# Mixer factors kept unsplit in DRAM, builder rows scaled on GpSimd, the pool pair's weights ahead of the norm of v, down's first activations in weight buffers

## The chip, the cores and the metric

One Trainium2 chip, of which the kernel uses one core. The time is device microseconds of one execution. Three runs of the kernel before took 2842.69, 2843.27 and 2844.00 us (median 2843.27).

## The reference

One decoder layer over 2048 prompt rows and 32 sample rows (8 sequences of 4), width D = 1024, all in f32:

```python
xn = rmsnorm(x)
proj = xn @ w_in        # u | v (512 each) | pool input (256) | queries (256) | 3 gates (1024 each)
u, v = split(gelu(a_part));  vn = layernorm(v)
br_a = (u * chunk_spatial(vn)) @ w_branch_a      # causal 128x128 mixing
br_b = pooled(pool_input) @ w_pool * scale @ w_branch_b   # windows 2, 4, 8, 16
br_c = cross_attn(q, mem_k, mem_v) @ w_branch_c  # 256 memory tokens
merged = sum(sigmoid(gate_i + b_i) * br_i)
h = x + rmsnorm(merged @ w_out)
g, up = split(rmsnorm(h) @ w_up)                 # 2816 each
out = h + rmsnorm((gelu(causal_conv3(g)) * up) @ w_down)
```

It also returns the memory keys and values, the pool and conv states and the normalised v of the sample rows.

## The kernel before

**Precision.** Each f32 operand is kept as a high and a low part (fp32r). `split_half` (L108) makes them: a ScalarE cast (L113) and a VectorE subtraction (L114). A product is then three matmuls: high x high, high x low, low x high. Weights arrive through `load_raw` (`rawp`, four buffers of 4 KB a partition) and are split into a ring of `u` tiles.

**Products in blocks.** The products with w_in and w_up are done as two-by-two block products with seven multiplications in place of eight (`blocks`, L392 and after; products 1, 6, 2, 7, 4, 5, 3). The right factors come from the weights: `right_factors` (L350) builds sums `sm` on VectorE (L359 to L364) and writes them to DRAM for later blocks, where `kept_factors` reads them. The left factors, named 1 to 8, are sums of transposed rows, made by a *builder* ahead of time. Product 1 leaves PSUM by a ScalarE copy to a tile `t` (L406), the others through VectorE (L410, L416).

**Stages.** The mixer handles four blocks of 512 prompt rows (block 1 also has the sample rows, `SB`), and for each: the values projection (`tok_mm`, L136 to L138, into `psv`), its GELU on ScalarE, the layer norm of v (bn_stats L633, bn_aggr L635, the reciprocal root on GpSimd L143 and L145, then L637 and L638 on VectorE), the pool pair (`pair(2 * AW)`, the first block product), pooling, queries and attention, the u part with its spatial gating (which reads the normalised v), and the gates: four steps with three gate products each and the branch products. Then `outproj` multiplies by w_out in two column halves of four rounds, each of which loads and splits a piece of w_out. After the four blocks come the up projection in two halves of the rows (its activations go to DRAM, `act`) and the down projection.

**The builder.** `mix_steps(b + 1)` and `ffn_items` are generators that `next(steps)` moves on once per gate product. An item (`pair_steps`) fetches pieces of two row tiles into a tile `fx` (SP's DMA, L247), scales each by its row's reciprocal root (L249, ScalarE), transposes them on TensorE (L233), takes the gains on ScalarE (L235, L236) and forms the sums on VectorE (L224 to L227). It then stores the factors to DRAM: three of them unsplit (`mf_`, L260), and the other five for the mixer as high and low parts (ScalarE copy `xh` L265, VectorE L266, four DMAs L268 and L270 to `md` and `m8`). There are 28 items for the mixer (24 of 128 rows, 4 of 16) and 36 for the feed-forward part. `load_block` loads a block's factors ahead of `outproj`: five tiles already split, and three that it splits (L304, L305). The tiles `fx`, `xh`, `t`, and others come from one pool, `w4`, of four buffers.

**Down.** Groups of two activations are loaded by `load_acts` into tiles `ar` of a pool `ra` (L1134), split (L1135 ScalarE, L1136 VectorE) and multiplied with w_down. The pool `ra` is opened when the pools of up are closed.

**Order.** A scheduler sets each engine's order when the program is built; engines then run in that order. One SP queue issues the loads and stores.

Of the kernel before, what the change touches and what calls it, by code (L numbers as in the profile page):

```python
# [50 lines left out]
def decoder_step(ctx: ExitStack, tc: tile.TileContext, A: dict, O: dict):  # L51
# [186 lines left out]
    def pair_steps(items, gains, spare=None):  # L238


        def fetch(e):
            rows, n, k = items[e][:3]
            pool, tag = (spare, "fx") if spare and e % 2 else (w4, "w4")
            f = pool.tile([P, D], F32, name="fx", tag=tag)
            for i, (src, r) in enumerate(rows):
                part = f[:n, 512:D].rearrange("p (h t c) -> p h t c", h=2, t=2)[:, :, i]
                DMA.dma_start(part, src.rearrange("p (h k c) -> p h k c", h=2, k=4)[:, :, k])  # L247
                if r is not None:
                    S.activation(part, part, AF.Copy, scale=r)  # L249
            return f  # L250

        nxt = fetch(0)
        yield
        for e, (rows, n, k, split, sums) in enumerate(items):
            f = nxt
            if e + 1 < len(items):
                nxt = fetch(e + 1)
            pair_cols(f, [f[:n, 512 + q * P:512 + (q + 1) * P] for q in (0, 2, 3, 1)], n, gains, k)
            pair_sums(f, n)
            DMA.dma_start(sums, f[:, 5 * n:8 * n].rearrange("p (i c) -> p i c", i=3))  # L260
            yield
            m = (4 + (len(split) > 1)) * n
            fa = f[:, 0:m]
            h = w4.tile([P, D], F32R, name="xh", tag="w4")[:, 0:m]
            S.copy(h, fa)  # L265
            V.tensor_tensor(fa.bitcast(F32R), fa, h.bitcast(F32), ALU.subtract)  # L266
            for hl, src in enumerate((h.bitcast(F32), fa)):
                DMA.dma_start(split[0][hl], src[:, 0:4 * n].rearrange("p (i c) -> p i c", i=4))  # L268
                if len(split) > 1:
                    DMA.dma_start(split[1][hl], src[:, 4 * n:5 * n])  # L270

    def ffn_items(b):
        s = b // 2
        pairs = [[(hd[r], rt[:, r:r + 1]) for r in (b * 4 + j, b * 4 + 2 + j)] + [P, (b % 2) * (xw[s] - 256) + j * P]
                 for j in range(2)]
        if b == 2:
            pairs.append([(hns[0:16], None), (hns[16:32], None), 16, 256])
        return [((r1, r2), n, k, [[xd[s][:, :, k // 2, hl, k % 2, c0:c0 + n] for hl in range(2)]],
                 xf[s][:, :, k, c0:c0 + n]) for r1, r2, n, c0 in pairs for k in range(4)]
# [8 lines left out]
    def mix_steps(b):  # L288

        for r1, r2, n, _ in mix_rows(b):  # L290
            for src, i in (r1, r2):
                xt = w4.tile([P, D], F32, name="xt", tag="w4")
                DMA.dma_start(xt[:n], src)
                row_rstd(xt[:n], n, rx[:n, i:i + 1])
            yield
        items = [([(src, rx[:n, i:i + 1]) for src, i in (r1, r2)], n, k,
                  [[md[b][:, k, hl, :, c0:c0 + n] for hl in range(2)], [m8[b][:, hl, k, c0:c0 + n] for hl in range(2)]],
                  mf_[b][:, :, k, c0:c0 + n]) for r1, r2, n, c0 in mix_rows(b) for k in range(4)]
        yield from pair_steps(items, gx)
# [7 lines left out]
    def load_block(b, own=None):  # L307

        X = own or {"A": []}
        if own is None:  # L310
            for k in range(4):
                X["A"].append(hb([P, 2, 4, mw[b]], name="xa"))
                DMA.dma_start(X["A"][k].bitcast(F32), md[b][:, k])
            X[8] = hb([P, 2, 4, mw[b]], name="x8")
            DMA.dma_start(X[8].bitcast(F32), m8[b])
        for i in (6, 5, 3):
# [3 lines left out]
        return X  # L320

    def factor(X, i):

        if "A" in X:
            return (lambda k, hl: X["A"][k][:, hl, XS.index(i)]) if i in XS else (lambda k, hl: X[i][:, hl, k])
        return lambda k, hl: X[i][k // 2][:, hl, k % 2]
# [127 lines left out]
    with ExitStack() as mctx, ExitStack() as m2ctx:  # L454
# [138 lines left out]
        def mixer(b, X, steps):  # L593
# [7 lines left out]
            def pair(c, each=None):  # L601
                W = kept_factors(c) if b else right_factors(w_in, c)
                for _, _, (h, *it) in all_blocks(W, X, [(0, w)], False, each):
                    yield (h, *it)
# [12 lines left out]
            for k in range(4):  # L617
                wr = raw3(v_first if b + k == 0 else load_raw(w_in[:, k:k + 5:4, AW:2 * AW]), 2)
                u = split_unit(wr)
                for ti, (h, c0, n) in enumerate(tts):  # L620
                    for k2 in range(2):
                        lh, ll = ((X["A"][k][:, hl, (0, 1)[k2] if h == 0 else 2] if h == 0 or k2 else X[8][:, hl, k])
                                  [:, c0:c0 + n] for hl in range(2))
# [5 lines left out]
            for ti, (h, c0, n) in enumerate(tts):  # L629
                vv = vn[:, ti] if n == P else w2.tile([P, NTB], F32, name="vg", tag="w2")[:n, 0:AW]  # L630
                S.activation(vv, psv[ti][:n], AF.Gelu_apprx_tanh)
                bs = stat.tile([P, 6], F32, name="bs", tag="bs")
                V.bn_stats(bs[:n], vv)  # L633
                ba = stat.tile([P, 2], F32, name="ba", tag="ba")
                V.bn_aggr(ba[:n], bs[:n])  # L635
                r = rstd_of(ba[:n, 1:2], n)
                V.scalar_tensor_tensor(vv, vv, ba[:n, 0:1], C["lng"][:n], ALU.subtract, ALU.mult)  # L637
                V.scalar_tensor_tensor(vv, vv, r, C["lnb"][:n], ALU.mult, ALU.add)  # L638
                vns.append(vv)
                if n < P:  # L640
                    DMA.dma_start(O["new_gmlp_v"].rearrange("l b t c -> (l b t) c")[16 * h:16 * h + 16], vv)
# [20 lines left out]
            for h, j, ps, add, op, sp in pair(2 * AW):  # L662
# [3 lines left out]
                for dst, sl, m in parts:  # L666
# [198 lines left out]
        def outproj(b, mg, steps=None, then=None):  # L865
# [10 lines left out]
            if steps:  # L876
                steps()
            ss2 = [stat.tile([P, 2], F32, name="sso", tag="sso") for _ in range(nt)]
            for ch in range(2):
# [111 lines left out]
        for k in range(4):  # L991
            f2 = hb([P, 2176], F32, name="fx")
            for j in range(2):
# [8 lines left out]
                DMA.dma_start(mf_[0][:, :, k, c0:c0 + P], f[:, 640:D].rearrange("p (i c) -> p i c", i=3))  # L1002
        X = load_block(0, X)
        for b in range(NB):
# [6 lines left out]
            if b < NB - 1:  # L1011
                nxt = {}
                outproj(b, mg, lambda: nxt.update(load_block(b + 1)))
                X = nxt
# [84 lines left out]
    with ExitStack() as fctx:  # L1099
# [19 lines left out]
        def down_all(s, pending):  # L1119
# [150 lines left out]
```

## Time and profile before

| | |
|---|---|
| median of three runs | 2843.27 us |
| the profiled execution | 2840.73 us |
| its span | 2838.9 us |
| mean granted TensorE clock | 0.985 |
| TensorE matmuls busy | 2727.1 us, 16833 instructions |
| VectorE busy | 2052.0 us, 3928 |
| ScalarE busy | 1310.6 us, 2510 |
| GpSimd busy | 111.8 us, 201 |
| HBM read, written | 336.32 MB, 104.18 MB |

The profile is of one execution. Engines are PE (TensorE's matmuls), PEld (its weight loads), DVE (VectorE), ACT (ScalarE), POOL (GpSimd) and SP (SyncE, which issues DMAs). A busy time is a sum over instructions; instructions of one engine overlap a little. In brackets behind a row of a timeline stands the idle time of the engine before it and what ended it. The block stages lie in the span as follows: the gates of blocks 0 to 3 at 195 to 325, 560 to 695, 895 to 1040 and 1195 to 1320 us; the pool pair and what follows the norm of v at 46 (block 0), 402 (1), 772 (2) and 1100 us (3); the output projection after block 0 and the values projection of block 1 at 325 to 402; up from 1450; down from 2317.

### The profile page before, as it was taken

Reading aid. Unit: us, or ns where it says so; the run is one execution under the profiler, and the core shown is the slowest. Engines: PE = TensorE matmul, PEld = TensorE weight load, DVE = VectorE, ACT = ScalarE, POOL = GpSimd, SP = SyncE. Lnnn points to the kernel's source line nnn. Section 1 sums busy time; section 2 is a strip of 40 time slices with the busy share of each in tenths; the row PEclk is TensorE's granted clock in tenths of the full one; section 3 lists DMA queues with packets and bytes.
Section 4 is the critical chain, followed back from the end, with each engine's and each line's share of the span. In section 5 each row is a group of like instructions: output and inputs, shape, how many; then the busy total and the mean of one; then the engine's idle time right before and its main releaser. Section 6 shows DMA issues by size and latency. Waiting matters only on the chain.

```text
span 2838.9 us, 45265 instructions
## 1 busy us (share of the span) xinstructions
PE 2727.1 (96%) x16833; PEld 2417.1 (85%) x16833; DVE 2052.0 (72%) x3928; ACT 1310.6 (46%) x2510; POOL 111.8 (4%) x201
## 2 busy tenths in 40 slices
PE   7999999999999999999999999999999989999998
PEld 5788878899889888989778788899999978888887
DVE  7788758477487667877587777767777757668665
ACT  5565446465466555756454433433333333115112
POOL 2010020000000001000000000000000000001001
PEclk9999999999999999999999999999999999999999
DMA  6457744586646774577744422442222244225312
GB/s 217 146 192 235 232 165 139 159 239 211 222 135 207 226 257 173 168 211 229 266 144 124 148 89 85 140 167 83 68 76 83 68 175 141 90 74 201 100 70 91
DMA packets 454639, 443.39 MB, mean 156 GB/s; under 512 B 32533, under 2 KB 385322, under 8 KB 450442
## 3 DMA queue, kind: packets, MB, share of 16 engines
q1 hardware_dynamic: 454418, 440.49, 47.9%
q8 instruction: 133, 2.18, 0.3%
q14 instruction: 88, 0.72, 0.1%
HBM read 336.32 MB, written 104.18 MB: 155 GB/s over the span
## 4 chain that ended last, share of the span: by engine, by line
issue 49%; PE 10%; DMA 2%; DVE 2%; ACT 1%; POOL 1%; SPq 0%; POOLq 0%; DVEq 0%; ACTq 0%
PE mm L388 5%; PE mm L136 1%; PE mm L138 1%; PE mm L137 1%; POOL rs L143 1%; PE mm L133 1%; PE mm L132 1%; PE mm L131 1%; DMA xd<-xh 1%; DMA fx<-hd 1%; POOL rs L145 1%; DMA m<-xh 0%; ACT tp L158 0%; DVE u L114 0%; ACT u L113 0%
## 5 line engine op out<-in xcount | busy, mean ns | idle before, releaser
L113 ACT CAST u<-raw 128x512 fp32r<-128x512 f32 x884 | 536.8, 620 | 949.6 <-PE mm L138 330.4
L388 PE MATMUL mm<-X,u 128*128 128x512 f32 (+2 forms) x5544 | 896.0, 323 | 7.5 <-ACT u L113 2.2
L388 PEld LDWEIGHTS mm<-X,u 128*128 128x128 f32 x5544 | 801.7, 189 | 93.7 <-DVE t L447 5.6
L114 DVE TENSOR_TENSOR u<-raw,u 128x512 fp32r<-128x512 f32 x884 | 597.8, 688 | 209.0 <-ACT u L113 203.0
L388 PE MATMUL mm<-xa,u 128*128 128x256 f32 (+1 forms) x3072 | 436.7, 294 | 21.5 <-ACT t L406 15.4
L388 PEld LDWEIGHTS mm<-xa,u 128*128 128x128 f32 x3072 | 399.0, 195 | 35.8 <-ACT t L406 20.6
L388 PE MATMUL mm<-xs,u 128*128 128x256 f32 (+1 forms) x2304 | 332.1, 291 | 20.0 <-ACT u L113 11.1
L388 PEld LDWEIGHTS mm<-xs,u 128*128 128x128 f32 x2304 | 300.3, 194 | 33.7 <-ACT u L113 14.0
L1148 DVE TENSOR_TENSOR Y<-Y,mm 128x512 f32<-128x512 f32 x268 | 183.2, 686 | 110.6 <-PE mm L138 109.9
L136 PE MATMUL mm<-u,a 128*128 128x512 f32 x616 | 242.9, 394 | 8.9 <-ACT a L1135 8.9
L138 PE MATMUL mm<-u,a 128*128 128x512 f32 x616 | 245.8, 399 | 0.0
L137 PE MATMUL mm<-u,a 128*128 128x512 f32 x616 | 244.9, 398 | 0.0
L136 PEld LDWEIGHTS mm<-u,a 128*128 128x128 f32 x616 | 117.8, 191 | 36.0 <-ACT a L1135 9.3
L137 PEld LDWEIGHTS mm<-u,a 128*128 128x128 f32 x616 | 116.5, 189 | 27.0
L138 PEld LDWEIGHTS mm<-u,a 128*128 128x128 f32 x616 | 116.3, 189 | 26.7 <-DVE a L1136 1.1
L114 DVE TENSOR_TENSOR u<-sm,u 128x512 fp32r<-128x512 f32 x120 | 82.8, 690 | 48.0 <-ACT u L113 46.5
L1072 DVE SCALAR_TENSOR_TENSOR d<-gE,vecs,d 128x1024 f32<-128x1024 f32 x88 | 112.7, 1280 | 5.7 <-ACT d L1070 5.2
L113 ACT CAST u<-sm 128x512 fp32r<-128x512 f32 x120 | 74.4, 620 | 86.2 <-PE mm L388 67.2
L416 DVE TENSOR_TENSOR t<-mm,t 128x256 f32<-128x256 f32 (+2 forms) x130 | 61.2, 471 | 63.3 <-PE mm L388 62.4
L143 POOL TENSOR_SCALAR rs<-ss 128x1 f32<-128x1 f32 (+2 forms) x57 | 33.8, 593 | 1734.6 <-ACT tp L158 1734.0
L136 PE MATMUL mm<-u,mg 128*128 128x512 f32 x224 | 88.8, 396 | 0.6 <-ACT mix L897 0.6
L138 PE MATMUL mm<-u,mg 128*128 128x512 f32 x224 | 88.2, 394 | 0.0
(300 smaller groups left out, 3764.0 us busy)
## 6 DMA issues: line engine op xcount, KB each, us to landing
raw<-in_w_in SPq DMA_DIRECT2D x96, 512.0 KB
raw<-ws SPq DMA_DIRECT2D x96, 512.0 KB
raw<-in_w_up SPq DMA_DIRECT2D x88, 512.0 KB
raw<-in_w_down SPq DMA_DIRECT2D x44, 512.0 KB
raw<-in_w_out SPq DMA_DIRECT2D x32, 512.0 KB
raw<-in_w_in SPq DMA_DIRECT2D x48, 256.0 KB
act<-d SPq DMA_DIRECT2D x22, 528.0 KB
ar<-act SPq DMA_DIRECT2D x22, 528.0 KB
```

The lines of the kernel that those rows point to most:

```text
L113: S.copy(uv[:, 0], src)
L114: V.tensor_tensor(uv[:, 1], src, uv[:, 0].bitcast(F32), ALU.subtract)
L131: T.matmul(ps, lhsT=uk[:, 0], rhs=xk(xT, k, 0, c0, n), start=i == 0, stop=False)
L132: T.matmul(ps, lhsT=uk[:, 0], rhs=xk(xT, k, 1, c0, n), start=False, stop=False)
L136: T.matmul(ps, lhsT=lh, rhs=wh, start=first, stop=False)
L137: T.matmul(ps, lhsT=lh, rhs=wl, start=False, stop=False)
L138: T.matmul(ps, lhsT=ll, rhs=wh, start=False, stop=last)
L143: G.tensor_scalar(r[:n], ms, more, EPS, ALU.add, ALU.add)
L388: T.matmul(ps, lhsT=u[:, wl, k], rhs=x(k, xl)[:, c0:c0 + n], start=not more and k + i == 0, stop=k + i == 5, skip_group_check=True)
L416: V.tensor_tensor(v7, pc, v, ALU.add)
L1072: V.scalar_tensor_tensor(d[j][:, 0:FSB], gE[j][:, k:k + FSB], cw(k, f), d[j][:, 0:FSB], ALU.mult, ALU.add)
L1148: return V.tensor_tensor(yd, yd, ps, ALU.add)
```

## The change

It has four parts.

*Factors unsplit in DRAM.* `md` holds all eight factors of a mixer block unsplit, in the order `MI`, and a mixer item stores them by one DMA (L259 of the new kernel). `xh` and its subtraction go for the mixer's items. `load_block` is now a generator: it loads the eight tiles one by one and splits each (L302, L303 of the new kernel); `outproj` moves it on after each of its eight weight splits, seven tiles early (six in block 1's), and the rest at its end.

*Row scale on GpSimd.* L249 becomes a GpSimd `tensor_scalar` (L247 of the new kernel): 112 instructions of 128 rows and 8 of 16.

*Pool pair ahead of the norm.* The pool pair's weights are taken before the norm of v, and the norm stands behind the pool pair in the program.

*Activations.* The first group of activations of down's first half is loaded through `load_raw` and not into `ra`.

```diff
-    md = [hdp.tile([P, 4, 2, 4, mw[b]], F32, name=f"md{b}") for b in range(NB)]
-    m8 = [hdp.tile([P, 2, 4, mw[b]], F32, name=f"m8{b}") for b in range(NB)]
-    mf_ = [hdp.tile([P, 3, 4, mw[b]], F32, name=f"mf{b}") for b in range(NB)]
+    md = [hdp.tile([P, 8, 4, mw[b]], F32, name=f"md{b}") for b in range(NB)]
...
-                    S.activation(part, part, AF.Copy, scale=r)
+                    G.tensor_scalar(part, part, r, None, ALU.mult)
...
+            if split is None:
+                DMA.dma_start(sums, f[:, 0:8 * n].rearrange("p (i c) -> p i c", i=8))
+                yield
+                continue
...
-    def load_block(b, own=None):
+    MI = (1, 2, 4, 7, 8, 5, 6, 3)
+
+    def load_block(b, X, order, early):
...
+        def load(i):
             X[i] = hb([P, 2, 4, mw[b]], name="xs")
-            DMA.dma_start(X[i][:, 1].bitcast(F32), mf_[b][:, XF.index(i)])
+            DMA.dma_start(X[i][:, 1].bitcast(F32), md[b][:, MI.index(i)])
+
+        for q, i in enumerate(order[:early]):
+            load(i)
+            if q:
+                split_sums(X[order[q - 1]])
+            yield
+        split_sums(X[order[early - 1]])
+        yield None
+        for i in order[early:]:
+            load(i)
+        for i in order[early:]:
             split_sums(X[i])
...
+            W_pool = weights(2 * AW)
+
+            def norm_v():
+                for (h, c0, n), vv in zip(tts, vns):
...
-            for h, j, ps, add, op, sp in pair(2 * AW):
+            for h, j, ps, add, op, sp in pair(2 * AW, None, W_pool):
...
+            norm_v()
             for i in range(2):
                 E = Ep[i]
...
                     u = split_unit(raw3(load_raw(w_out[:, 2 * kh:2 * kh + 2, ch * 512:(ch + 1) * 512]), 2))
+                    next(steps, None)
...
+            for _ in steps:
+                pass
             if then:
                 then()
...
-                outproj(b, mg, lambda: nxt.update(load_block(b + 1)))
-                X = nxt
+                X = {}
+                outproj(b, mg, load_block(b + 1, X, (1, 2, 8, 4, 6, 7, 5, 3), 6 if b == SB else 7))
...
-                    r = ra.tile([P, FSB + NS], F32, name="ar", tag="ar")
+                    r = load_raw() if s + gidx == 0 else ra.tile([P, FSB + NS], F32, name="ar", tag="ar")
```

How the order moves, at three places. An order row has the line, the operation, out<-in and the shape; the numbers in a name are the scheduler's. First VectorE's order in block 2 at the norm of v (`bs`, `ba`, `vn`), beside which the residual rows of the block before (`rows`, `hnr`) are finished. Before:

```order
L633 BN_STATS bs<-vn 128x6
L635 BN_AGGR ba<-bs 128x2
L637 SCALAR_TENSOR_TENSOR vn<-vn,ba,lng 128x512
L193 SCALAR_TENSOR_TENSOR rows<-rows,rs_8549,post_row 32x1024
L633 BN_STATS bs<-vn 128x6
L195 TENSOR_TENSOR rows<-rows,rr 32x1024
L635 BN_AGGR ba<-bs 128x2
L633 BN_STATS bs<-vn 128x6
L637 SCALAR_TENSOR_TENSOR vn<-vn,ba,lng 128x512
L635 BN_AGGR ba<-bs 128x2
L633 BN_STATS bs<-vn 128x6
L924 TENSOR_SCALAR hnr<-rows,rs_8562 32x1024
```

Now:

```order
L644 BN_STATS bs<-vn 128x6
L646 BN_AGGR ba<-bs 128x2
L648 SCALAR_TENSOR_TENSOR vn<-vn,ba,lng 128x512
L193 SCALAR_TENSOR_TENSOR rows<-rows,rs_8421,post_row 32x1024
L644 BN_STATS bs<-vn 128x6
L195 TENSOR_TENSOR rows<-rows,rr 32x1024
L114 TENSOR_TENSOR u<-raw,u 128x512 x3
L936 TENSOR_SCALAR hnr<-rows,rs_8434 32x1024
L414 TENSOR_TENSOR t_8610<-mm,t_8610 128x256
L649 SCALAR_TENSOR_TENSOR vn<-vn,rs_8713,lnb 128x512
L420 TENSOR_TENSOR t_8610<-mm,t_8610 128x256
```

Three weight splits and the first product's way out of PSUM (L414) now stand ahead of most of the norm.

Second, the SP queue in the gates of block 0, where the builder's loads (`fx<-in_x_prompt`), its stores and the weights' loads (`raw<-in_w_in`) share one order. Before:

```order
L260 DMA mf_120<-fx 384x1x128
L100 DMA raw<-in_w_in 128x8x128
L268 DMA md_112<-xh 128x4x128
L270 DMA m_116<-xh 128x128
L268 DMA md_112<-fx 128x4x128
L270 DMA m_116<-fx 128x128
L100 DMA raw<-in_w_in 128x8x128
L247 DMA fx<-in_x_prompt 128x2x128 x2
```

Now:

```order
L245 DMA fx<-in_x_prompt 128x2x128 x4
L100 DMA raw<-in_w_in 128x8x128 x4
L377 DMA ws_2659<-raw 128x512
L375 DMA ws_2659<-sm 128x1024
L376 DMA ws_2659<-raw 128x512
L100 DMA raw<-in_w_in 128x8x128
L259 DMA md_112<-fx 1024x1x128 x2
L100 DMA raw<-in_w_in 128x8x128
```

The loads of two items stand together ahead of the weights, and an item has one store where it had five.

Third, ScalarE's order at the end of up, where `d` is the gated activation, `a` the high part of a loaded one and `Y` down's sum. Before:

```order
L1080 ACTIVATE d<-d,vecs 128x1056
L113 CAST u<-raw 128x512
L406 COPY t_24533<-mm 128x256
L113 CAST u<-raw 128x512 x10
L1135 CAST a<-ar 128x1024 x2
L1147 COPY Y<-mm 128x512 x13
```

Now:

```order
L1092 ACTIVATE d<-d,vecs 128x1056
L1147 CAST a<-raw 128x1024
L113 CAST u<-raw 128x512
L410 COPY t_24359<-mm 128x256
L1147 CAST a<-raw 128x1024
L113 CAST u<-raw 128x512 x5
L1159 COPY Y<-mm 128x512
```

The two casts of the first activations stand ahead of, and right behind, up's last copy out of PSUM, where they stood behind ten more weight casts. On TensorE three of down's matmuls now stand ahead of up's last twelve products.

## Rows read from the trace of the kernel before

**Rows 1.** The page's first part: busy time and share of each engine.

```profile
PE 2727.1 (96%) x16833; PEld 2417.1 (85%) x16833; DVE 2052.0 (72%) x3928; ACT 1310.6 (46%) x2510; POOL 111.8 (4%) x201
```

**Rows 2.** Table by stretch: us, busy time (instructions) by engine, clock, DMA share, GB/s.

```profile
195.00:325.00 130.00, 118.79 (x834) 109.25 (x833) 103.49 (x210) 74.28 (x153) 0.10 (x1) 0.97 0.68 206
...
325.00:402.00 77.00, 76.60 (x340) 60.15 (x339) 41.63 (x65) 34.40 (x71) 5.96 (x15) 1.00 0.70 249
...
402.00:446.00 44.00, 40.27 (x250) 33.38 (x250) 38.28 (x89) 21.05 (x46) 10.72 (x15) 1.00 0.32 104
...
560.00:695.00 135.00, 129.97 (x1022) 128.19 (x1021) 103.18 (x239) 84.55 (x171) 0.19 (x2) 1.00 0.77 227
...
772.00:812.00 40.00, 35.90 (x223) 31.96 (x221) 30.51 (x53) 23.26 (x52) 8.33 (x18) 0.91 0.41 134
...
895.00:1040.00 145.00, 136.90 (x959) 126.86 (x958) 108.17 (x214) 88.20 (x168) 0.20 (x2) 0.99 0.74 222
...
1195.00:1320.00 125.00, 118.93 (x825) 109.74 (x824) 92.09 (x186) 74.06 (x147) 0.00 (x0) 0.99 0.73 218
...
2300.00:2335.00 35.00, 24.66 (x147) 21.09 (x146) 17.65 (x38) 12.03 (x19) 0.00 (x0) 0.80 0.67 241
```

**Rows 3.** Timeline between up and down: start, us, engine, what, [idle before, releaser].

```profile
2319.43 1.94 SPq L1134 DMA_DIRECT2D ar<-act  x3
...
2324.56 1.04 ACT L1135 CAST a<-ar 128x1024 fp32r<-128x1024 f32 x1 [1.76 <-DMA ar<-act]
...
2325.65 0.80 PE L136 MATMUL mm<-u,a 128*128 128x512 f32 x1 [8.91 <-ACT a L1135]
...
2332.51 0.40 PE L136 MATMUL mm<-u,a 128*128 128x512 f32 x1
...
2334.36 0.40 PE L138 MATMUL mm<-u,a 128*128 128x512 f32 x1
```

**Rows 4.** Timeline of block 0, at the pool pair, ACT and PE.

```profile
51.59 0.62 ACT L113 CAST u<-sm 128x512 fp32r<-128x512 f32 x1 [3.32 <-DVE sm L361]
...
52.26 0.80 PE L388 MATMUL mm<-xs,u 128*128 128x256 f32 x2 [4.40 <-ACT u L113]
```

**Rows 5.** Timeline of block 2, at the pool pair, PE.

```profile
792.29 2.44 PE L388 MATMUL mm<-xa,u 128*128 128x256 f32 x12 [1.95 <-ACT t L406]
...
796.51 2.50 PE L388 MATMUL mm<-xa,u 128*128 128x256 f32 x10 [0.52 <-DVE u L114]
```

**Rows 6.** PE's waits (us, times, longest): gates of block 0, 2, 3; last, whole span.

```profile
PE tp L233 <- ACT fx L249: 6.4, 6, 2.2
...
PE mm L388 <- ACT u L113: 4.0, 5, 2.0
...
PE mm L388 <- ACT t L406: 6.9, 6, 2.3
...
PE mm L388 <- ACT t L406: 5.2, 6, 2.1
...
PE tp L233 <- ACT fx L249: 12.6, 10, 3.9
```

**Rows 7.** Timeline of block 0, POOL.

```profile
43.65 0.23 POOL L143 TENSOR_SCALAR rs<-ba 128x1 f32<-128x1 f32 x1 [5.42 <-DVE ba L635]
...
49.69 1.91 POOL L143 TENSOR_SCALAR rs<-ba 128x1 f32<-128x1 f32 x1 [3.05 <-DVE ba L635]
```

**Rows 8.** By source line: VectorE's splits (lowest/median/highest ns, first and last start us).

```profile
L114 DVE TENSOR_TENSOR u<-raw,u x884: 659/687/698, 13.4 to 2781.7; 128x512 fp32r<-128x512 f32 x177
```

**Rows 9.** Groups by line and shape: busy us, mean ns, idle before, releaser.

```profile
L249 ACT ACTIVATE fx<-fx,rx 128x256 f32<-128x256 f32 x48 | 23.3, 506 | 14.2 <-DMA fx<-in_x_prompt 11.3 <-issue 2.4 <-ACT u L113 0.2
...
L265 ACT CAST xh<-fx 128x640 fp32r<-128x640 f32 x24 | 17.5, 728 | 3.6 <-DMA m<-fx 2.6 <-ACT fx L236 0.4 <-DMA m<-xh 0.2
...
L304 ACT CAST xs<-xs 128x1024 fp32r<-128x1024 f32 x9 | 9.6, 1066 | 10.0 <-DMA xs<-mf 10.0
...
L492 POOL TENSOR_SCALAR_AFFINE_SELECT wsn<-wsn 128x512 f32<-128x512 f32 x1 | 1.8, 1764 | 7.6 <-DMA wsn<-in_w_spatial 7.6
```

More of the change, by code (lines that the diff above doesn't have):

```diff
@@ L277, in ffn_items @@
             pairs.append([(hns[0:16], None), (hns[16:32], None), 16, 256])
-        return [((r1, r2), n, k, [[xd[s][:, :, k // 2, hl, k % 2, c0:c0 + n] for hl in range(2)]],
+        return [((r1, r2), n, k, [xd[s][:, :, k // 2, hl, k % 2, c0:c0 + n] for hl in range(2)],
                  xf[s][:, :, k, c0:c0 + n]) for r1, r2, n, c0 in pairs for k in range(4)]
@@ L295, in mix_steps @@
             yield
-        items = [([(src, rx[:n, i:i + 1]) for src, i in (r1, r2)], n, k,
-                  [[md[b][:, k, hl, :, c0:c0 + n] for hl in range(2)], [m8[b][:, hl, k, c0:c0 + n] for hl in range(2)]],
-                  mf_[b][:, :, k, c0:c0 + n]) for r1, r2, n, c0 in mix_rows(b) for k in range(4)]
+        items = [([(src, rx[:n, i:i + 1]) for src, i in (r1, r2)], n, k, None, md[b][:, :, k, c0:c0 + n])
+                 for r1, r2, n, c0 in mix_rows(b) for k in range(4)]
         yield from pair_steps(items, gx)
@@ L305, in split_sums @@
         V.tensor_tensor(lo, lo.bitcast(F32), hi.bitcast(F32), ALU.subtract)
-    def load_block(b, own=None):
[L309 to L316, printed above, removed]
-            X[i] = hb([P, 2, 4, mw[b]], name="xs")
-            DMA.dma_start(X[i][:, 1].bitcast(F32), mf_[b][:, XF.index(i)])
+    MI = (1, 2, 4, 7, 8, 5, 6, 3)
+    def load_block(b, X, order, early):
+        def load(i):
+            X[i] = hb([P, 2, 4, mw[b]], name="xs")
+            DMA.dma_start(X[i][:, 1].bitcast(F32), md[b][:, MI.index(i)])
[9 more added lines that the diff above has]
+        for i in order[early:]:
             split_sums(X[i])
-        return X
     def factor(X, i):
-        if "A" in X:
-            return (lambda k, hl: X["A"][k][:, hl, XS.index(i)]) if i in XS else (lambda k, hl: X[i][:, hl, k])
-        return lambda k, hl: X[i][k // 2][:, hl, k % 2]
+        if isinstance(X.get(i), list):
+            return lambda k, hl: X[i][k // 2][:, hl, k % 2]
+        return (lambda k, hl: X[i][:, hl, k]) if i in X else lambda k, hl: X["A"][k][:, hl, XS.index(i)]
     upool = {}
@@ L599, in mixer, with weights, pair @@
             tts = [(tt // 2, (tt % 2) * P, P) for tt in range(NTT)] + ([(0, 256, 16), (1, 256, 16)] if smp else [])
-            def pair(c, each=None):
-                W = kept_factors(c) if b else right_factors(w_in, c)
+            def weights(c):
+                return kept_factors(c) if b else right_factors(w_in, c)
+            def pair(c, each=None, W=None):
+                W = W or weights(c)
                 for _, _, (h, *it) in all_blocks(W, X, [(0, w)], False, each):
@@ L621, in mixer @@
                     for k2 in range(2):
-                        lh, ll = ((X["A"][k][:, hl, (0, 1)[k2] if h == 0 else 2] if h == 0 or k2 else X[8][:, hl, k])
-                                  [:, c0:c0 + n] for hl in range(2))
+                        lh, ll = (factor(X, ((1, 2), (8, 4))[h][k2])(k, hl)[:, c0:c0 + n] for hl in range(2))
                         tok_mm(psv[ti][:n], lh, ll, u[k2][:, 0, 0], u[k2][:, 1, 0], k + k2 == 0, k + k2 == 4)
@@ L863, in mixer, with outproj @@
             return mg
-        def outproj(b, mg, steps=None, then=None):
+        def outproj(b, mg, steps=iter(()), then=None):
             smp = b == SB
@@ L1001, in decoder_step @@
                     V.tensor_tensor(dst[:, 1], src, dst[:, 0].bitcast(F32), ALU.subtract)
-                DMA.dma_start(mf_[0][:, :, k, c0:c0 + P], f[:, 640:D].rearrange("p (i c) -> p i c", i=3))
-        X = load_block(0, X)
+                DMA.dma_start(md[0][:, 5:8, k, c0:c0 + P], f[:, 640:D].rearrange("p (i c) -> p i c", i=3))
+        for _ in load_block(0, X, (6, 5, 3), 3):
+            pass
         for b in range(NB):
```

32 lines of the change are left out of this document (13 added, 19 removed).

## The prediction

> **What bounds the kernel now.** The page's first part comes first: TensorE counts as busy for 96% of the span, VectorE for 72%, ScalarE for 46% and GpSimd for 4% [rows 1]. The reader is to see that the matmuls are the bound and that the change, which removes none of them, can win only TensorE's idle time and the time in which its matmuls run at a lower clock. So the second view is the table by stretch [rows 2], cut at the stages: in the gates of the four blocks TensorE idles for 130 - 118.79 = 11.2, 5.0, 8.1 and 6.1 us (30.4 together), around the pool pair 3.7 us in block 1 and 4.1 in block 2, during the output projection after block 0 and the values projection behind it 0.4, and at the border between up and down 10.3 at a mean granted clock of 0.80. The third view tells, for the largest of these holes, what TensorE waited for: the timeline where one gap holds it [rows 3 to 5], the list of waits where many do [rows 6].
>
> The sum is made against the profiled execution, 2840.7 us with a span of 2838.9. The median of the runs is 2843.3, 2.5 higher; the forecast is given on that scale.
>
> **Step 1, first activations of down in weight buffers: -12 us.** Down's first matmul waits 8.91 us for `a L1135` [rows 3]. That cast waits for a transfer that SP issues only at 2319.4, because the pool `ra` is opened after up's pools are closed. The buffers of `load_raw` exist from the start, and the order shows the loads behind the store of activation 18, the casts among up's last weight casts and three of down's matmuls ahead of up's last twelve products. So the wait goes. Behind it the first 15 matmuls, from 2325.65 to 2332.51, take 6.86 us; the next eight start at 0.231 us each ((2334.36 - 2332.51) / 8), at which 15 take 3.5. The matmuls are 0.63 us long at first and 0.40 later [rows 3], and the stretch has the lower granted clock [rows 2], behind an idle TensorE. Without the idle stretch I expect no fall: 8.9 + 3.4 = 12.3, taken as -12. Ends: -9 if the slow start stays, -13.5 if some of the rest of the 10.3 idle goes too. The cover is up's last products: in the old run two activations took 5.1 us from SP's issue at 2319.43 to the first cast at 2324.56, and here they start far before up's end. The loads take two of the four raw buffers; if the weights of down come late for that, the next wait is a `u` cast's. The second group's activations still use `ra`; over them lie 96 matmuls of the first group, 96 x 0.231 = 22 us.
>
> **Step 2, norm of v behind the pool pair: -7 us.** In block 0 the pool pair's second product waits 4.40 us for a `u` cast, which waited 3.32 us for `sm L361` on VectorE [rows 4]. In the old order norm operations of two tiles stand in front of `sm`; in the new it stands straight behind the copies of the spatial weights. So ScalarE's 3.32 us should nearly go: I take -3. In block 2 the pool pair waits 1.95 us for `t L406` and 0.52 for a `u` split [rows 5], and the stretch's mean clock is 0.91 [rows 2]; the order now has three splits ahead of the norm. The 1.95 is ScalarE's and stays; with the clock I take -2. In block 1 the idle time is 3.7 us [rows 2], in block 3 of the same kind; VectorE is busy for 38.28 of 44 us there, so the norm only moves behind what the pair needs and remains to be done before the gating of v: -1 each. Sum -7. Ends: -2, where the later norm makes TensorE wait before the spatial gating instead, and -13, where nearly all of the 3.7 + 4.1 + 4.4 us and that of block 3 go.
>
> **Step 3, gates: -10 us.** Three edits meet here. Of the 30.4 us idle, 22.5 are put down to four waits: 6.4 for the scaled rows (`fx L249`), 4.0 for a `u` cast, and 6.9 + 5.2 for `t L406` [rows 6]. All four are ScalarE's, in order behind L249, which itself idles 14.2 us for the rows' transfer [rows 9]. With the scale on GpSimd, ScalarE no longer stands still for a transfer. The hi copies of the mixer's items, 24 x 728 ns = 17.5 us of ScalarE [rows 9], go too, with the `xh` buffers that `t` waited for; both lay beside matmuls and count for nothing themselves. SP has the rows' loads earlier, two items at once. What remains is the chain transfer, scale, transposes, now with GpSimd's scale in it. No GpSimd operation of this size is in the trace: below lies 0.23 us for a 128x1 operation [rows 7], above 1.76 us for one that reads 128x512 [rows 9]. I take half of that, 0.9, since it has half the columns, against 0.507 on ScalarE: two per item cost 0.8 us more, hidden where rows come a gate ahead. I count 45% of the 22.5, so -10. Ends: -22, and +8, where each of the six waits of block 0 grows by 1.91 - 0.51 = 1.4 us (the 1.91 is the stretched operation of [rows 7]).
>
> **Step 4, splits moved into the output projection: +2 us.** Five more tiles are split per block, 15 x 1.066 us = 16 us on ScalarE and a little more on VectorE. In the stretch of the output projection and the values projection ScalarE is busy for 34.4 of 77 us, VectorE for 41.6 [rows 2], so the work fits. One cast per round stands ahead of a weight cast and waits for its transfer: over the nine of now that is 10.0 us, 1.1 each [rows 9]. One round of weights is four row tiles x 3 x 2 = 24 matmuls x 0.231 = 5.5 us, which covers 1.07 + 1.1. The last splits are drained at the end, where the next values projection is near: I take +0.7 per block, +2, with ends 0 and +6. SP moves less than before.
>
> Sum: -12 - 7 - 10 + 2 = -27, so 2813.7 against 2840.7, and **2816 us** on the median's scale.
>
> **Rivals.** *A, the gates give nothing.* GpSimd's latency takes what ScalarE gives. For it: GpSimd's one-column operation took 1.91 us beside a busy VectorE and 0.23 beside an idle moment [rows 7]. Against it: the rows are now fetched earlier. Then -12 - 7 + 2 = -17: 2826.
>
> *B, slower: GpSimd is starved.* If a two-input VectorE operation running back to back holds GpSimd off, both scales of an item take 1.91 us for 0.51, 2.8 more. TensorE waited for the scale in ten items [rows 6]; if each of these ends last again, 10 x 2.8 = +28 instead of -10: -17 + 28 = +11, so 2854. It decides from (12 + 7 - 2) / 10 = 1.7 us per item. For it: VectorE is busy for 75 to 80% of the gates [rows 2]. Against it: VectorE's 884 splits run within 659 to 698 ns [rows 8], so it is never the one that gives way, but its gaps are a quarter of the time.
>
> A rule speaks for A and B: the Trainium skill, "SBUF — State Buffer", section "SBUF: two separate sides", calls the port pair that VectorE and GpSimd share an exclusive lock; a VectorE operation with two SBUF inputs and a GpSimd operation that reads SBUF block each other for a whole instruction, whoever starts first. The rows agree for GpSimd (0.23 against 1.91 us) and not for VectorE (698 ns at most), though GpSimd has done nothing large in the old kernel. By the rule VectorE would lose up to 0.9 us at each of 120 scales; where VectorE is three quarters busy that fits into its idle time, and by the rule alone the sum would be A's.
>
> *C, more than forecast.* All of the four ScalarE waits but 2 us go, and the pool pairs' waits almost wholly: -13 - 13 - 20 + 0 = -46: 2797.
>
> **How the numbers follow.** Forecast 0.60, A 0.20, C 0.10, B 0.10. A measurement can tell about 0.2% (5.7 us) from no change, so faster means below 2837.6, slower above 2849. The forecast, A and C lie below; of A's low gains (steps 1 and 2 at their small ends and +6 in step 4 give -9 - 2 + 6 = -5, 2838) some fall within the bound. Faster 0.86, same 0.05, slower 0.09. The range runs from C's 2796 to those 2838; it leaves out B and the far ends of C.
>
> **What would show it.** Right: no gap over 1 us between up's last and down's first matmul, and 0.40 us matmuls from the start; block 0's 4.4 us gone; in the gates no wait for `t L410` of a us or more, total idle of the four stretches near 20; the GpSimd scale near 0.9 us. Wrong: a GpSimd scale of 1.5 us or more with waits of the transposes for it beyond 12.6 us in sum [rows 6]; waits for `xs` or `u` in the output projection of over 2 us per block; a new wait of TensorE ahead of the spatial gating for `vn`.

## The result and the profile after

The changed kernel takes 2797.46 us (median of four runs, 2796.86 to 2799.83) against 2842.98 for the kernel before: a ratio of 0.9846 with a 95% interval of 0.9829 to 0.9864, or 45.5 us less. The time lies in the range, near its low end; the forecast of 2816 was 18.5 us too high. The profiled execution of the changed kernel took 2799.83 us, 40.9 less than that of before.

The first part of the page of the changed kernel, beside [rows 1]:

```profile
PE 2711.8 (97%) x16833; PEld 2408.8 (86%) x16833; DVE 2059.0 (74%) x3915; ACT 1261.8 (45%) x2377; POOL 247.9 (9%) x321
```

TensorE does the same 16833 matmuls in 15.3 us less of busy time; the other 25.5 of the 40.8 us by which the span fell are idle time. ScalarE is busy for 49 us less, with the new splits already counted, and GpSimd for 136 us more.

Where the time went is read by stage. The table takes each stage from its first matmul to the next stage's first, as the timeline has them; "pool pair to u" is the stretch from the pool pair's first product to the gates' first.

| us | before | after | difference | forecast |
|---|---|---|---|---|
| gates, blocks 0 to 3 | 194.0, 222.9, 185.2, 182.4 | 179.4, 218.1, 173.1, 177.7 | -36.2 | -10 |
| pool pair to u, blocks 0 to 3 | 97.8, 69.1, 69.9, 67.3 | 100.5, 70.6, 71.4, 67.3 | +5.7 | -7 |
| output and values projections | | | -1.6 | +2 |
| up and down | 923.9 + 513.2 | 915.3 + 511.8 | -10.0 | -12 |
| start, up to the first pool pair | 46.2 | 47.5 | +1.3 | 0 |

The table by stretch of the kernel before, cut at these borders (gates of block 0 and of block 2 in two halves each, then block 0 from the pool pair's end to the gates):

```profile
144.00:240.10 96.10, 89.67 (x622) 82.53 (x621) 79.62 (x151) 58.77 (x125) 8.79 (x12) 0.98 0.67 208
240.10:338.00 97.90, 91.07 (x631) 83.46 (x630) 82.12 (x167) 56.14 (x115) 0.20 (x2) 0.98 0.70 207
...
855.30:945.60 90.30, 87.55 (x627) 81.25 (x626) 67.73 (x128) 57.64 (x117) 6.17 (x8) 1.00 0.69 209
945.60:1040.50 94.90, 88.75 (x626) 82.75 (x625) 70.83 (x141) 57.34 (x111) 0.20 (x2) 0.98 0.73 217
...
64.70:144.00 79.30, 71.59 (x485) 57.11 (x485) 59.42 (x123) 43.29 (x98) 1.97 (x4) 0.96 0.45 154
```

And of the changed kernel, the same stretches:

```profile
148.00:237.90 89.90, 87.05 (x624) 80.93 (x622) 77.85 (x146) 52.12 (x110) 21.85 (x24) 1.00 0.68 216
237.90:327.40 89.50, 87.24 (x631) 81.06 (x629) 78.04 (x158) 47.34 (x94) 14.16 (x14) 1.00 0.71 222
...
842.10:928.80 86.70, 86.70 (x628) 81.33 (x626) 66.38 (x124) 50.64 (x103) 21.52 (x22) 1.00 0.69 210
928.80:1015.20 86.40, 86.40 (x627) 81.04 (x625) 69.40 (x137) 50.45 (x94) 10.47 (x12) 1.00 0.72 221
...
60.10:148.00 87.90, 75.46 (x486) 60.32 (x485) 63.32 (x130) 43.57 (x98) 2.77 (x6) 0.88 0.42 142
```

The gates of block 2 now run with no idle time of TensorE at all, where 2.75 + 6.15 = 8.9 us stood. In block 0 the idle time fell by 8.2 us, and the busy time by 6.4 more (180.7 to 174.3). The granted clock rose there from 0.98 to 1.00, which over 194 us is worth some 3 to 4 of these 6.4, an estimate; the rest is not explained by it. The last row is the other side: behind the pool pair of block 0 TensorE idles 12.4 us where it was 7.7, at a granted clock of 0.88 in place of 0.96.

TensorE's waits over the whole span of the changed kernel (us, times, longest), beside [rows 6]:

```profile
PE mm L392 <- ACT t L410: 9.8, 7, 3.6
PE tp L231 <- POOL fx L247: 8.7, 7, 3.5
PE tp L729 <- DVE po L595: 7.7, 2, 5.3
PE mm L392 <- ACT u L113: 6.2, 5, 2.2
...
PE tp L729 <- DVE po L591: 4.3, 2, 3.6
```

The seven waits for GpSimd's scale all lie in up. The waits of `tp L729`, the product of the pooled means, have grown to 12.0 us together, from 2.7 for the same product in the kernel before:

```profile
PE tp L718 <- DVE po L587: 1.5, 2, 0.8
...
PE tp L718 <- DVE po L591: 1.2, 1, 1.2
```

Between up and down the timeline of the changed kernel reads, beside [rows 3]:

```profile
2276.88 1.05 ACT L1147 CAST a<-raw 128x1024 fp32r<-128x1024 f32 x1 [1.44 <-PE mm L392]
...
2286.28 0.40 PE L136 MATMUL mm<-u,a 128*128 128x512 f32 x1
...
2286.97 1.66 PE L392 MATMUL mm<-X,u 128*128 128x256 f32 x12
...
2288.48 0.40 PE L136 MATMUL mm<-u,a 128*128 128x512 f32 x1
```

The first cast is done 8 us before down's first matmul, which has neither a wait nor the slow start; up's last products follow it.

### The profile page after: what moved, and what is told of

Same layout as the page of the kernel before. It is cut to its first block, busy times and chain, and to the rows that moved or that the text cites. A ratio compares the mean times of both kernels' runs of the same rounds, so it can differ in the third digit from the quotient of the medians.

```text
span 2798.1 us, 45245 instructions
## 1 busy us (share of the span) xinstructions
PE 2711.8 (97%) x16833; PEld 2408.8 (86%) x16833; DVE 2059.0 (74%) x3915; ACT 1261.8 (45%) x2377; POOL 247.9 (9%) x321
## 3 DMA queue, kind: packets, MB, share of 16 engines
HBM read 328.29 MB, written 96.15 MB: 152 GB/s over the span
## 4 chain that ended last, share of the span: by engine, by line
PE 39%; issue 9%; POOL 1%; DVE 1%; DMA 0%; ACT 0%; SPq 0%; POOLq 0%; DVEq 0%; ACTq 0%
PE mm L392 30%; PE mm L138 3%; PE mm L137 3%; PE mm L136 3%; POOL rs L143 0%; POOL rs L145 0%; PE tp L231 0%; POOL fx L247 0%; DVE Y L1160 0%; DVE X L303 0%; DVE Y L193 0%; DMA fx<-hd 0%; DMA xd<-fx 0%; ACT tp L158 0%; DVE u L114 0%
## 5 line engine op out<-in xcount | busy, mean ns | idle before, releaser
L392 PE MATMUL mm<-xs,u 128*128 128x256 f32 (+1 forms) x4608 | 619.7, 291 | 16.7 <-ACT t L410 6.1
L392 PEld LDWEIGHTS mm<-xs,u 128*128 128x128 f32 x4608 | 583.5, 193 | 36.8 <-ACT u L113 7.9
L247 POOL TENSOR_SCALAR fx<-fx,rt 128x256 f32<-128x256 f32 x64 | 74.4, 1171 | 421.3 <-DMA fx<-hd 266.1
L114 DVE TENSOR_TENSOR u<-sm,u 128x512 fp32r<-128x512 f32 x120 | 82.5, 688 | 39.6 <-ACT u L113 38.8
L392 PE MATMUL mm<-xa,u 128*128 128x256 f32 x768 | 108.8, 293 | 1.8 <-DVE u L114 1.6
L392 PEld LDWEIGHTS mm<-xa,u 128*128 128x128 f32 x768 | 99.3, 197 | 5.7 <-DVE u L114 2.7
L136 PE MATMUL mm<-u,mg 128*128 128x512 f32 x224 | 88.7, 396 | 0.0
```

What stands on the lines that cost most here:

```text
L114: V.tensor_tensor(uv[:, 1], src, uv[:, 0].bitcast(F32), ALU.subtract)
L136: T.matmul(ps, lhsT=lh, rhs=wh, start=first, stop=False)
L247: G.tensor_scalar(part, part, r, None, ALU.mult)
L392: T.matmul(ps, lhsT=u[:, wl, k], rhs=x(k, xl)[:, c0:c0 + n], start=not more and k + i == 0, stop=k + i == 5, skip_group_check=True)
```

## The experiments

Twelve kernels were run. Each is told by its ratio to the kernel before, with the 95% interval, where the changed kernel has 0.9846 (0.9829 to 0.9864), and by the stage lengths of its profile. "The gates" are the sum over four blocks: 784.5 us before, 748.3 after.

### e1: the norm of v back

```diff
-            W_pool = weights(2 * AW)
-            def norm_v():
+                bs = stat.tile([P, 6], F32, name="bs", tag="bs")
...
-            norm_v()
```

> The changed kernel with the norm of v put back ahead of the pool pair. Theory (the moved norm only moves the wait): in the changed kernel the four pool pairs are 10.5 us shorter than before, but the stretch behind them (pooling, queries, attention, u part) is 16.2 us longer, with TensorE waiting 12.0 us for the pooled means. So this kernel should be 3 to 7 us faster than the changed one (about 2792), and those waits for pooled means should fall below 3 us. Rival (the move pays 7 us, as forecast): about 2804.

Measured: 2795.44 us, ratio 0.9838 (0.9815 to 0.9861). By the whole time that is 2 us faster than the changed kernel, less than the theory's 3 to 7, and the two are not told apart. By stage they are: pool pair to u takes 304.3 us, as before (304.1), against 309.8, and TensorE waits 2.5 us for the pooled means; the gates stay at 747.5. By the stage lengths the move has not paid, it has cost 5.5 us.

### e2: the row scale back on ScalarE

```diff
-                    G.tensor_scalar(part, part, r, None, ALU.mult)
+                    S.activation(part, part, AF.Copy, scale=r)
```

> The changed kernel with the builder's row scale back on ScalarE. Theory (the gates' gain of 36.5 us comes mostly from ScalarE no longer standing still behind the row scale): the gates become longer by 20 to 30 us, 2817 to 2827, with TensorE's waits for t and for the scaled rows back at 20 us or more. Rival (the gain comes from the unsplit factors, which free ScalarE, VectorE, the w4 buffers and SP): at most 8 us slower than the changed kernel, below 2806.

Measured: 2819.07 us, ratio 0.9916 (0.9890 to 0.9942), 21.6 us slower than the changed kernel, as the theory has it. But not in all blocks: the gates are 178.7, 226.6, 181.7 and 185.0 us. Block 0 keeps its whole gain; blocks 1 to 3 lose 8.5, 8.6 and 7.3. TensorE's waits over the whole span, and in block 3's gates a wait of ScalarE:

```profile
PE mm L392 <- ACT t L410: 19.7, 17, 3.3
PE mm L392 <- DVE gt L620: 9.6, 13, 1.5
...
ACT fx L247 <- DMA fx<-hd: 14.8, 10, 3.1
```

In the gates of blocks 1, 2 and 3 ScalarE stands still before the scale, for the rows' transfer, for 6.8, 11.8 and 14.8 us; the changed kernel has no such wait.

In up, where the builder runs on, the scale on ScalarE is better: 911.7 us against 915.3.

### e3: the factors split again

```diff
-    md = [hdp.tile([P, 8, 4, mw[b]], F32, name=f"md{b}") for b in range(NB)]
+    md = [hdp.tile([P, 4, 2, 4, mw[b]], F32, name=f"md{b}") for b in range(NB)]
...
+            h = w4.tile([P, D], F32R, name="xh", tag="w4")[:, 0:m]
+            S.copy(h, fa)
```

> The changed kernel with the mixer factors again stored split (hi copy, subtraction and five stores per item; load of five split tiles). Theory (the row scale carries the gain): 5 to 12 us slower than the changed kernel, 2803 to 2810, in block gates alone. Rival (the unsplit factors carry it): 20 us or more slower, above 2817.

Measured: 2835.98 us, ratio 0.9976 (0.9961 to 0.9990). The theory, that the scale carries the gain, fell, and the rival held: 38.5 us are lost. The gates are 199.8, 222.4, 185.2 and 177.6 us: blocks 0 to 2 no better than before, block 0 worse by 5.8; only block 3, which builds no mixer items, keeps its gain. The largest wait of this kernel:

```profile
PE tp L233 <- POOL fx L249: 27.1, 22, 4.7
```

More than half of these 27.1 us, 14.7 in 11 waits, lie in block 0's gates. The reason there is in the timeline. The same item of block 0, before (SP's fetch, the scale, the transposes):

```profile
214.29 1.25 SPq L247 DMA_DIRECT2D fx<-in_x_prompt  x2
...
217.70 0.91 ACT L249 ACTIVATE fx<-fx,rx 128x256 f32<-128x256 f32 x2
...
218.26 0.84 PE L233 MATMUL tp<-ident,fx 128*128 128x128 f32 x4 [1.10 <-ACT fx L249]
```

in e3:

```profile
213.41 1.25 SPq L247 DMA_DIRECT2D fx<-in_x_prompt  x2
...
216.21 2.19 POOL L249 TENSOR_SCALAR fx<-fx,rx 128x256 f32<-128x256 f32 x2 [12.10 <-DMA fx<-in_x_prompt]
...
217.56 0.44 PE L233 MATMUL tp<-ident,fx 128*128 128x128 f32 x2 [1.20 <-POOL fx L249]
...
218.46 0.44 PE L233 MATMUL tp<-ident,fx 128*128 128x128 f32 x2 [0.46 <-POOL fx L249]
```

and in the changed kernel:

```profile
208.67 1.26 SPq L245 DMA_DIRECT2D fx<-in_x_prompt  x2
...
211.60 2.38 POOL L247 TENSOR_SCALAR fx<-fx,rx 128x256 f32<-128x256 f32 x2 [13.07 <-DMA fx<-in_x_prompt]
```

There its transposes come at 237.1 us, 28 us behind the fetch. Counted over the timeline, 6 of block 0's 12 items were fetched less than 6.5 us ahead of their transposes before and in e3; in the changed kernel none was, the shortest lead being 13 us. So the theory changed: the unsplit factors need no `xh` and set the item's tile free at once, the fetch comes early, and then the length of GpSimd's scale does not matter.

That is the account of block 0 alone. In block 1 no item of e3 was fetched less than 8 us ahead and in block 2 only two of 12 were less than 6.5, and TensorE waits there for the scale for nothing and for 0.8 us. Yet block 2 loses 12.1 us against the changed kernel. What TensorE waits for there is VectorE's way out of PSUM (`gt`), 7.9 us, and the longest of these waits follows one of ScalarE for a weight transfer, which stands in the SP queue behind the item's four stores of split factors:

```profile
921.64 0.38 SPq L268 DMA_DIRECT2D md<-xh  x1
...
923.90 2.08 SPq L100 DMA_DIRECT2D raw<-ws  x1
...
927.76 1.66 ACT L113 CAST u<-raw 128x512 fp32r<-128x512 f32 x3 [5.37 <-DMA raw<-ws]
...
931.03 1.26 PE L388 MATMUL mm<-xs,u 128*128 128x256 f32 x6 [3.81 <-DVE gt L616]
```

Over block 2's gates ScalarE waits 20.2 us for weights in e3 and 6.0 in the changed kernel. The profile shows no other wait of SP ahead of that load, so that the stores delay the weights is the likely cause; no run here shows it alone.

### e4: down's first activations in their own pool

```diff
-                    r = load_raw() if s + gidx == 0 else ra.tile([P, FSB + NS], F32, name="ar", tag="ar")
+                    r = ra.tile([P, FSB + NS], F32, name="ar", tag="ar")
```

> The changed kernel with down's first activations again in their own pool. Theory (the wait and the slow start behind it are both paid by this part): 11 to 13 us slower, 2808 to 2811, with a wait of 8 to 9 us ahead of down's first matmul. Rival (the slow clock stays in any case): 8 to 9.5 us slower, 2805 to 2807.

Measured: 2814.05 us, ratio 0.9900 (0.9877 to 0.9923); 16.6 us slower by the medians, which is above both expectations, and 9.6 by the spans of the profiles. By stage up takes 928.8 us against 915.3, 13.5 more; the gates are the same. The timeline has both parts of it, the wait and the slow matmuls:

```profile
2295.86 0.79 PE L136 MATMUL mm<-u,a 128*128 128x512 f32 x1 [8.73 <-ACT a L1147]
...
2296.45 0.63 PE L137 MATMUL mm<-u,a 128*128 128x512 f32 x1
```

### e5: the buffer held, without the work

```diff
-                DMA.dma_start(sums, f[:, 0:8 * n].rearrange("p (i c) -> p i c", i=8))
+                DMA.dma_start(sums[:, 1:8], f[:, n:8 * n].rearrange("p (i c) -> p i c", i=7))
                 yield
+                h = w4.tile([P, D], F32, name="xh", tag="w4")[:, 0:n]
+                S.copy(h, f[:, 0:n])
+                DMA.dma_start(sums[:, 0:1], h.rearrange("p (i c) -> p i c", i=1))
                 continue
```

> The changed kernel, in which a mixer item again holds a second tile of w4 into its next step: seven factors are stored at once, and the first is copied (128 columns on ScalarE, no subtraction) into a tile of its own after the step and stored from there. The work is almost that of the changed kernel; only the buffers are held as before. Theory (the unsplit factors gain because the rows of the next items can be fetched 10 to 28 us ahead, where a held buffer leaves 3 to 4 us for half of block 0's items): 20 to 35 us slower than the changed kernel, 2817 to 2832, with transposes waiting over 20 us for GpSimd's scale. Rival (the copy of 640 columns, the subtraction and the five stores were the cost): at most 8 us slower, below 2806.

Measured: 2816.94 us, ratio 0.9916 (0.9901 to 0.9931), 19.5 us slower than the changed kernel: at the theory's low end, far from the rival's. (A copy of 128 columns and a second store per item remain.) The gates are 762.5 us, 14.2 of the 36.7 that e3 lost. The held tile brought the short lead back for two of block 0's items only (6.3 and 6.4 us), not for six as in e3; TensorE waits 6.0 us for the scale there, and 14.9 over the span, not the 20 that were expected:

```profile
PE tp L231 <- POOL fx L247: 14.9, 8, 3.2
```

### e9: the work, without the held buffer

```diff
+                fa = f[:, 0:5 * n]
+                S.copy(fa, fa)
+                V.tensor_tensor(fa, fa, fa, ALU.max)
-                DMA.dma_start(sums, f[:, 0:8 * n].rearrange("p (i c) -> p i c", i=8))
+                for c0, c1 in ((0, 2), (2, 4), (4, 5), (5, 7), (7, 8)):
+                    DMA.dma_start(sums[:, c0:c1], f[:, c0 * n:c1 * n].rearrange("p (i c) -> p i c", i=c1 - c0))
```

> The changed kernel with the old work put back at each mixer item but no tile held: a ScalarE copy of the first five factors onto themselves, a VectorE maximum of them with themselves, and five stores in place of one; all factors stay unsplit and the item's tile is free after its stores. With e5 it divides what the unsplit factors are worth in the gates (36.8 us in e3, of which e5 gave back 14.2 by the held buffer alone). Theory (the buffers and the fetch are most of it; the work lies beside matmuls): at most 8 us slower than the changed kernel, below 2806. Rival (the rest, some 20 us, is this work on ScalarE, VectorE and SP): 2813 to 2822.

Measured: 2806.07 us, ratio 0.9870 (0.9850 to 0.9890), 8.6 us slower: just above the theory's bound and well short of the rival. The gates are 754.4 us, 6.1 more. So of e3's 36.7 us the buffers as e5 holds them make 14.2 and the work alone 6.1. The remaining 16 are open: e5 shortens the lead of fewer items than e3 does, the two may need each other, and neither has e3's larger transfers (104.18 MB written and 336.32 read, against 96.15 and 328.29 in e5, e9 and the changed kernel). No run here took that apart.

### e6: the scale twice

```diff
                     G.tensor_scalar(part, part, r, None, ALU.mult)
+                    G.tensor_scalar(part, part, 1.0, None, ALU.mult)
```

> The changed kernel with a second GpSimd multiplication (by 1.0) behind each row scale, so that an item's chain is some 2.3 us longer and GpSimd does 240 operations in place of 120. Theory (with the fetch far ahead GpSimd's time is hidden in the mixer blocks; only some seven items of the feed-forward part are fetched under 6.5 us ahead): 5 to 16 us slower, 2803 to 2813. Rival (GpSimd's latency is paid at every item, or VectorE is held by it): 64 items x 2.3 us, more than 50 us slower, above 2847.

Measured: 2811.89 us, ratio 0.9901 (0.9883 to 0.9918), 14.4 us slower, as the theory has it. The gates are 180.0, 218.0, 173.2 and 184.6 us: nothing in blocks 0 to 2, 6.9 in block 3, and up takes 923.0 us, 7.7 more. In blocks 0 to 2, where the fetch leads by 11 us or more, twice the scale is free.

### e7 and e8: the norm of v further back

```diff
-            norm_v()
             for i in range(2):
                 E = Ep[i]
...
                 pooled.append(po)
+            norm_v()
```

> The changed kernel with the norm of v one step further back, behind the pooled means. Theory (in the changed kernel VectorE does the norm ahead of the pooled means, for which TensorE waits 12.0 us): the pool pairs stay short and those waits fall below 4 us: 2785 to 2791. Rival (VectorE is full there and only passes the wait on): within 4 us of the changed kernel, with a new wait ahead of the spatial gating.

Measured: 2803.46 us, ratio 0.9870 (0.9851 to 0.9888): slower than the changed kernel by 6 us by the medians (the two intervals overlap), outside both expectations. Pool pair to u takes 313.7 us. In the order that the scheduler made, most of the norm still stands ahead of the pooled means on VectorE, and the waits for them are still there (10.9 us together).

```diff
-            norm_v()
             for i in range(2):
                 E = Ep[i]
...
+            norm_v()
             if b == 0:
                 stage_mem()
```

> The changed kernel with the norm of v behind the queries, ahead of the attention. Theory: as with the norm behind the pooled means, 2783 to 2790, since nothing reads the normalised v before the spatial gating. Rival: the norm now stands in VectorE's way in the attention, and the time is within 4 us of the changed kernel.

Measured: 2795.68 us, ratio 0.9839 (0.9820 to 0.9858), within the rival's 4 us of the changed kernel by its median. Pool pair to u takes 303.8 us: the 5.7 us are back, and not more than that. The wait for the pooled means is 0.3 us in block 0; one for `xt L536`, a row of the memory that VectorE norms, has come:

```profile
PE tp L541 <- DVE xt L536: 6.5, 1, 6.5
```

### e10: the best of the parts

```diff
-                    G.tensor_scalar(part, part, r, None, ALU.mult)
+                    if spare:
+                        S.activation(part, part, AF.Copy, scale=r)
+                    else:
+                        G.tensor_scalar(part, part, r, None, ALU.mult)
```

and the norm as in e8; `spare` is set in up alone.

> The norm of v behind the queries (e8), and in the up projection alone, where the builder still has split items and seven of them are fetched under 6.5 us ahead, the row scale back on ScalarE. Theory (GpSimd's scale costs up 3.6 to 4.9 us, by e2 and e4, and the norm's place 5.5): 2786 to 2791, faster than the changed kernel by 6 to 11 us. Rival (up's waits are for the rows' transfer): as e8, 2793 to 2797.

Measured: 2785.52 us, ratio 0.9800 (0.9781 to 0.9819): faster than the changed kernel, with intervals that do not overlap. Up takes 907.7 us in place of 915.3, more of a gain than the theory's 3.6 to 4.9; pool pair to u takes 307.3, between e8's 303.8 and the changed kernel's 309.8, less than the 5.5 expected. It is the fastest of all the kernels here, half a us below the theory's range.

### e11 and e12: scale alone, factors alone

The kernel before with only the line of e2 changed (e11), and with only the diff's hunks on `md`, `load_block` and `outproj` (e12).

> The kernel before with the row scale on GpSimd and nothing else. Theory (GpSimd's scale pays only where the rows are fetched far ahead, which needs the unsplit factors): between 5 us faster and 8 us slower than the kernel before, with TensorE waiting over 20 us for the scale. Rival (the scale on GpSimd pays by itself, by freeing ScalarE): 15 us faster or more.

> The kernel before with the factors unsplit in DRAM and nothing else. Theory (the fetch comes earlier, but ScalarE still stands still behind the scale in blocks 1 to 3): 10 to 20 us faster than the kernel before, the gain being in block 0's gates. Rival (the two parts add up): 30 us faster or more.

Measured: e11 takes 2846.37 us, ratio 1.0013 (1.0002 to 1.0023), e12 2827.31, ratio 0.9951 (0.9936 to 0.9967). Both came as their theories have it. The scale alone costs some 4 us: in block 0 the gates grow from 194.0 to 202.0, in up 923.9 to 930.0, and TensorE waits

```profile
PE tp L233 <- POOL fx L249: 26.1, 22, 4.1
```

The factors alone save 14 us (0.0049 x 2843): block 0's gates shrink to 179.2, the full gain, and in blocks 1 to 3 `t` is waited for again (17.4 us over the span). In the gates the scale alone saves 2.1 us and the factors alone 14.7, together 16.8, and the two in one kernel 36.2. By block:

| gates, us | block 0 | block 1 | block 2 | block 3 |
|---|---|---|---|---|
| before | 194.0 | 222.9 | 185.2 | 182.4 |
| scale alone (e11) | 202.0 | 219.9 | 182.5 | 178.0 |
| factors alone (e12) | 179.2 | 225.9 | 180.3 | 184.4 |
| both (changed kernel) | 179.4 | 218.1 | 173.1 | 177.7 |

The factors alone give block 0 its whole gain and the scale alone gives block 3 nearly its own; blocks 1 and 2 gain fully only with both.

## Why the prediction was right and wrong

**Sign and range** held: the kernel is faster, and 2797 lies between 2796 and 2838. The size was nearly that of rival C (2797), but not by C's terms: C had -13, -13, -20 and 0 for the four steps; it was -10, +6, -36 and -2 (and +1 at the start). That the time lies in the range is in part luck: an error of 26 us in step 3 and one of 13 the other way in step 2 cancel in part.

**Step 1 was right.** Forecast -12; undoing it alone gives 13.5 us by stage (e4), or 9.9 where the scale is on ScalarE (up and down of e12 against e2), and the first of down's matmuls are 0.40 us long, as named. That up and down together show only 10.0 has another cause as well, which the forecast put into the gates alone: GpSimd's scale makes up slower, by 6.1 us where it comes alone (930.0 against 923.9) and by 3.6 in the changed kernel against e2.

**Step 2 was wrong in sign.** The step that failed is "the norm only moves behind what the pair needs and remains to be done before the gating of v: -1 each": the sum prices what comes behind the pair at nothing, in the four blocks alike. From the pool pair to the gates blocks 0 to 3 were forecast at -3, -1, -2 and -1 and came out at +2.7, +1.5, +1.5 and 0.0. Block 0's 4.40 us went, and the four pool pairs are 10.5 us shorter, more than forecast; but what comes behind them is 16.2 longer. The pooled means stand between norm and gating, VectorE makes them, and in TensorE's order their product stands in the middle of the next pair. In block 1 the profile had the sign of it: VectorE is busy for 38.28 of 44 us there [rows 2]. An engine that is this full passes the wait on, and where the norm is moved further (e8) the stretch returns to 303.8, what it was with the norm ahead. Four kernels with the norm ahead have 304 to 305 us (before, e1, e11, e12), and seven with it in the change's place 308 to 310.

**Step 3 was right in sign and too small.** The terms that failed are "I count 45% of the 22.5" and the reading of the three edits as one sum. First, 19 of the 22.5 us went where the forecast had under half: in block 0 0.6 us of waits for a `u` cast are left, in block 3 2.7 for `t`. The reason that the forecast gave is borne out in blocks 1 to 3: with the scale back on ScalarE (e2) that engine stands still again for the rows' transfer, and the gates lose 8.5, 8.6 and 7.3 us. Second, the gap is not all that a wait costs: of the 36.2 us 24.2 are idle time (39.6 before, 15.4 after, summed over the table by stretch) and 12.0 are less busy time of the same matmuls. Step 1 had counted such a term, the lower clock, at its own place, and step 3 had not. By the mean granted clock of the four gates (0.98, 0.97, 0.99, 0.99 before; 1.00, 0.97, 1.00, 0.99 now) some 5 to 6 of the 12 are the lower clock, an estimate; the rest stays open. Third, the buffers: the forecast said that the copies "lay beside matmuls and count for nothing themselves" and named the freed `xh` tiles only as what `t` waited for. In block 0 it is with the tiles freed that the fetch leads by some 13 us or more, and with that lead the scale on GpSimd is hidden (e3, e5, e6, e11, e12). The single store has a part in it: with five stores and the old work but no held tile (e9) the shortest lead there is 6.7 us, and TensorE still waits for no scale. In blocks 1 and 2, where most items led by 7 us or more already, the unsplit factors are worth 4.3 and 12.1 us beside GpSimd's scale (e3); there the waits point to the SP queue's stores and weights and to the tiles that `t` needs, and which of them it is stays open.

**Step 4** was forecast +2 and came out at -1.6: the 27 casts of `xs` wait 16.5 us for their loads, 0.6 each in place of the 1.1 assumed, and TensorE waits for none of them.

**Rival B** came close in the kernels that lack the unsplit factors: 22 waits of TensorE for GpSimd's scale, 26.1 us (e11), of which 14.8 lie in block 0's gates, which lost 8 us. It did not come in the changed kernel's gates. **Rival A's** rule, the lock of the Trainium skill's "SBUF — State Buffer" page (section "SBUF: two separate sides"), is weighed in the last section.

## What to carry to other kernels

In block 0 the producer's buffers set how far ahead it could fetch, and the lead decided whether the length of its steps counted: look for the time from a fetch to its use, item by item, before pricing a slower engine in the chain. Two edits can be worth little apart and much together, as where one makes the lead that hides the other's latency; take such a sum apart by stage, since the same total can have another reason in each. Moving work behind a wait on an engine that is already full moves the wait; look at what that engine has to do next.

## What the runs showed of the hardware

GpSimd's scale of 128x256 took 1.16 us on average in the changed kernel, not the 0.9 of the estimate. By line, with the lowest, median and highest duration in ns:

```profile
L247 POOL TENSOR_SCALAR fx<-fx,rt x64: 918/1078/2007, 633.3 to 1587.6; 128x256 f32<-128x256 f32 x64
...
L114 DVE TENSOR_TENSOR u<-raw,u x884: 654/685/926, 14.0 to 2740.8; 128x512 fp32r<-128x512 f32 x177
```

Four scales met no VectorE operation at all and took 913 to 922 ns; the 103 that ran beside two-input VectorE operations (`TENSOR_TENSOR`) alone took 1144 on average and up to 1814. VectorE's splits went up to 926 ns, where they were at most 698 before [rows 8]; the 87 that overlap a scale average 709 ns, the other 917 686 (both with the splits of `sm`). So by these durations both engines are slowed beside each other, but VectorE by 23 ns on average and a quarter of a us at most. The exclusive lock of the Trainium skill's "SBUF — State Buffer" page (section "SBUF: two separate sides") would have VectorE wait for a whole instruction of GpSimd; here that is 0.9 us, so the trace does not agree on VectorE's side. For GpSimd, with up to 1.1 us more, it does.
